# A hybrid decoder layer on one core: branches, output projection and second feed-forward product by seven half-size products each

## Chip, cores and metric

The kernel runs on one core of one Trainium2 chip. The metric is the device time of one execution in microseconds. TensorE is called PE here, VectorE DVE, ScalarE ACT, GpSimd POOL, and SyncE, which issues most DMAs, SP.

## What is computed

One decoder layer over 1024 tokens of width 1024, in float32, batch 1. One input projection feeds two causal mixers (a Mamba-2 scan and an xLSTM matrix memory). Each mixer gives 2048 channels per token. Cut to what the change touches:

```python
y_a = ssd_branch(...)                   # 1024 x 2048, RMS-normed
y_b = mlstm_branch(...)                 # 1024 x 2048, times its output gate
ba, bb = y_a @ w_branch_ssd, y_b @ w_branch_mlstm       # 2048 x 1024 weights
m = sigmoid(g_a) * ba + sigmoid(g_b) * bb
x1 = x + gate1 * (m @ w_out)                            # 1024 x 1024 weight
h = rms_norm(x1) * (1 + scale) + shift
u, g = split(h @ w_ffn_in)                              # width 2816 each
out = rms_norm(x1 + gate2 * ((silu(g) * u) @ w_ffn_out)) * final_norm_w
```

Every factor of a product is held as a pair: a high part rounded to the fast float32 format of PE (f32r) and a low part, the rest. A product takes three matmuls: high x high, high x low, low x high.

## The kernel before, in words

A tile is 128 partitions by 512 or 1024 elements. One matmul has a 128x128 stationary operand and 512 columns, and adds into one of eight PSUM banks of 128x512.

The program has these stages. **Mixers**: the input projection (`gemm`, L276 to L287, 48 matmuls for 128 columns of the weight), convolutions and scans. Their results go to DRAM as `u_d` and `y_d`, the gates (`gate_tile`, L309) as `tg_d`. During the last part, the four heads of the mLSTM scan (L696 to L708), gemms of gates and of the next head stand between the scan's steps.

**Branches and output projection**, in two halves of 512 tokens (L1005 to L1011). For a half, `half_merge` (L805) runs `branch` (L776) twice: for each of 16 blocks of 128 input channels it loads a tile of tokens and a row block of the weight, splits both into pairs, and issues 24 matmuls into all eight banks (L795); `kouter` (L742) interleaves the last two blocks so that the banks end one after the other. DVE then reads each bank, gates it and adds the branches up. `half_out` (L840) multiplies the merged half by `w_out` through `tokgemm` (L828, matmuls L835), and `residual` (L753) adds the rows of x. In the second half of tokens the first branch runs ahead of the operands `f0`, `h0` of the first half (L1007 to L1009).

**Seam**: `feat` (L855) transposes the normed rows, and `ffn_inputs` (L869) forms the sums and differences of the two token halves that the next product needs, 20 pairs in all.

**First feed-forward product** (`ffn1`, L890): for each of 22 blocks `j` of 128 columns, gate and up part together are a 2x2 block product that is computed with seven half-size products (two "head" products `p1`, `p2` and five of sums; matmuls L903). POOL adds up the weights (`wsum`, L894), ACT and DVE split the sums into pairs (`split_pair`, L860: a cast at L863 and a subtraction at L864). The products go to `act_d` in DRAM.

**Second feed-forward product** (`ffn2`, L971): two halves of tokens, each a `tokgemm` over 22 blocks of `act_d` rows and `w_ffn_out` rows, then residual, norm and store.

A scheduler that simulates the program sets the order of the instructions of each engine; tile pools (name, tag, number of buffers) bound how far one part runs ahead of another. All loads in these stages stand on SP's queue, the stores of the mixers and of `act_d` on POOL's.

## Time and profile before

| | us |
|---|---|
| median of 3 runs | 2723.82 |
| lowest and highest run | 2723.11, 2727.63 |
| profiled execution, its own time | 2723.68 |
| its span in the profile | 2722.0 |
| busy in the span: PE | 2605.1 (96%) |
| busy: DVE, ACT, POOL | 1495.7, 1029.5, 434.8 |
| moved by DMA | 323.8 MB, 119 GB/s on average |

The busy time of an engine is the time in which at least one of its instructions runs. Matmuls overlap one another, so PE's busy time is not the sum of their durations. The stretches of the rows below are cut where a stage's first or last matmul stands in the trace: mixers to 1517.4 us, branches and output projection to 1989.0, seam to 2048.3, first feed-forward product to 2460.5, second to 2705.4, tail to 2722.0.

### The profile page before, as it was taken

To read this page: it belongs to the slowest core of one execution; us is meant where nothing else is said; L and a number is where in the kernel's file an instruction comes from. 1 tells how busy PE (TensorE), PEld (TensorE's weight loads), DVE (VectorE), ACT (ScalarE), POOL (GpSimd) and SP (SyncE) were. 2 spreads that over 40 slices of the span, in tenths; PEclk is the share of its full clock that TensorE was granted. 3 is DMA by queue.
4 is the path that set the end of the run, shared out by engine and by line. 5 is a ranking of instruction groups with operands and counts; after the bars stand their busy time and mean duration, and the time that the engine had idled before them with its cause. 6 is when DMAs were issued, how large, how long until landed. Compare 5 with 4: busy or idle time off the path is not lost.

```text
span 2722.0 us, 34219 instructions
## 1 busy us (share of the span) xinstructions
PE 2605.1 (96%) x13279; PEld 2174.1 (80%) x13279; DVE 1495.7 (55%) x2280; ACT 1029.5 (38%) x1785; POOL 434.8 (16%) x410
## 2 busy tenths in 40 slices
...
GB/s 198 100 82 113 104 116 78 113 143 99 133 129 140 88 117 88 61 72 99 55 99 101 162 173 187 177 173 199 136 78 83 78 87 82 82 79 218 137 208 94
DMA packets 261099, 323.80 MB, mean 119 GB/s; under 512 B 16288, under 2 KB 180480, under 8 KB 260936
## 3 DMA queue, kind: packets, MB, share of 16 engines
...
q8 instruction: 104, 1.70, 0.3%
q14 instruction: 59, 0.48, 0.1%
...
## 4 chain that ended last, share of the span: by engine, by line
PE 77%; DVE 7%; DMA 6%; issue 5%; ACT 3%; POOL 3%; SPq 0%; DVEq 0%; POOLq 0%; ACTq 0%
PE mm L284 31%; PE mm L560 7%; PE n L903 6%; PE n L835 5%; PE n L795 4%; PE mm L835 3%; PE sc L835 3%; PE sc L903 3%; PE mm L903 3%; PE n L612 2%; PE mm L795 2%; PE sc L795 2%; DMA raw<-in_w_ffn_in_dram 2%; PE n L630 1%; DMA ab<-acs_d 1%
## 5 line engine op out<-in xcount | busy, mean ns | idle before, releaser
L122 DVE TENSOR_TENSOR wl<-raw,wh 128x1024 fp32r<-128x1024 f32 x250 | 314.6, 1260 | 511.1 <-PE mm L284 155.1
L284 PE MATMUL mm<-hh,wh 128*128 128x512 f32 x1392 | 551.1, 396 | 4.5 <-ACT xf L296 4.3
L284 PE MATMUL mm<-hh,wl 128*128 128x512 f32 x1392 | 549.8, 395 | 0.0
L284 PE MATMUL mm<-hl,wh 128*128 128x512 f32 x1392 | 549.5, 395 | 0.0
L121 ACT CAST wh<-raw 128x1024 fp32r<-128x1024 f32 x250 | 262.1, 1048 | 656.9 <-PE n L835 118.1
L284 PEld LDWEIGHTS mm<-hh,wh 128*128 128x128 f32 x1392 | 262.9, 189 | 57.7 <-ACT xf L296 5.0
L284 PEld LDWEIGHTS mm<-hh,wl 128*128 128x128 f32 x1392 | 262.7, 189 | 51.7 <-issue 0.5
L284 PEld LDWEIGHTS mm<-hl,wh 128*128 128x128 f32 x1392 | 263.0, 189 | 50.8 <-issue 0.2
L304 DVE SCALAR_TENSOR_TENSOR xf<-cr,pk,xf 128x1023 f32<-128x1023 f32 (+2 forms) x120 | 161.9, 1351 | 22.7 <-ACT xf L296 21.6
L795 PE MATMUL n<-us,wh 128*128 128x512 f32 x512 | 159.6, 394 | 7.1 <-DVE am L813 7.1
L903 PE MATMUL n<-t,sw 128*128 128x512 f32 x552 | 140.9, 402 | 16.6 <-ACT sw L863 14.5
L903 PEld LDWEIGHTS n<-t,sw 128*128 128x128 f32 x552 | 105.3, 191 | 43.8 <-ACT sw L863 15.0
L864 DVE TENSOR_TENSOR sw<-ws,sw 128x512 fp32r<-128x512 f32 x88 | 75.9, 867 | 88.2 <-ACT sw L863 87.9
L795 PEld LDWEIGHTS n<-us,wh 128*128 128x128 f32 x512 | 96.8, 190 | 27.9 <-DVE am L813 7.8
L863 ACT CAST sw<-ws 128x512 fp32r<-128x512 f32 x88 | 54.0, 619 | 166.8 <-POOL ws L896 116.4
L835 PE MATMUL n<-wh,ap 128*128 128x512 f32 x352 | 115.1, 389 | 0.0
L464 ACT ACTIVATE ab<-ab,gsum 128x128 f32<-128x128 f32 x256 | 78.5, 389 | 83.2 <-DMA ab<-acs_d 77.7
L795 PE MATMUL n<-us,wl 128*128 128x512 f32 x256 | 99.7, 392 | 0.0
L520 POOL TENSOR_TENSOR Y<-Y,tz 128x512 f32<-128x512 f32 x14 | 33.3, 2396 | 386.3 <-DVE Y L501 222.1
L187 POOL TENSOR_TENSOR sm<-sm,mhalf 128x1 f32<-128x1 f32 x32 | 17.8, 558 | 479.5 <-DVE sm L186 479.5
L896 POOL TENSOR_TENSOR ws<-raw 128x512 f32<-128x512 f32 x44 | 60.0, 1363 | 181.7 <-DMA raw<-in_w_ffn_in_dram 171.0
L560 PE MATMUL mm<-wh,hh 128*128 128x256 f32 x512 | 82.3, 283 | 0.0
(359 smaller groups left out, 4962.4 us busy)
## 6 DMA issues: line engine op xcount, KB each, us to landing
raw<-in_w_in_dram SPq DMA_DIRECT2D x104, 512.0 KB, 4.0
raw<-in_w_ffn_in_dram SPq DMA_DIRECT2D x44, 512.0 KB, 3.8
raw<-in_w_ffn_out_dram SPq DMA_DIRECT2D x44, 512.0 KB, 3.6
raw<-in_w_ada_dram SPq DMA_DIRECT2D x40, 512.0 KB, 3.8
tg_d<-tz POOLq DMA_DIRECT2D x64, 256.0 KB, 2.7
ab<-acs_d SPq DMA_DIRECT2D x32, 512.0 KB, 4.0
raw<-in_w_branch_ssd_dram SPq DMA_DIRECT2D x32, 512.0 KB, 3.7
tgl<-tg_d SPq DMA_DIRECT2D x64, 256.0 KB, 2.8
```

Of the source, the lines that this page charges most:

```text
L121: A.copy(wh, raw)
L122: V.tensor_tensor(wl, raw, f(wh), SUB)
L284: T.matmul(ps, lhsT=ww[:, k, :], rhs=xx[:, halves(hf)], start=n == 0, stop=n == 23)
L304: V.scalar_tensor_tensor(dst[:, sh:], cr[:, :S - sh], cw[:, 3 - sh, ti:ti + 1], dst[:, sh:], MUL, ADD)
L464: A.activation(ab[q][:, e, c], ab[q][:, e, c], AF.Relu, scale=-1.0, bias=acs_t[:, 4 * q + c, h0 + e:h0 + e + 1])
L560: T.matmul(ps[:, c], lhsT=hT[k][x_][:, sl], rhs=ws[k // 4][w_][:, k % 4], start=n == 0, stop=n == 23)
L612: T.matmul(nv(i), lhsT=l_, rhs=r_, start=n == 0, stop=n == len(ops) - 1)
L795: T.matmul(bk[j], lhsT=l_[:, js], rhs=us[:, r_], start=first and n == 0, stop=last and n == 2)
L835: T.matmul(bk[i], lhsT=at[:, l_, tt * P:(tt + 1) * P], rhs=r_[:, halves(nh)], start=first and n == 0, stop=last and n == 2)
L864: e.tensor_tensor(m[:, 1], t, f(m[:, 0]), SUB)
L896: G.tensor_tensor(s, x, y, op)
L903: T.matmul(bank, lhsT=ww[:, k, :], rhs=b[k][:, r_], start=k == 0 and n == 0, stop=k == 3 and n == 2)
```

## The change

The two branches, the output projection and the second feed-forward product are each computed for all 1024 tokens at once as a 2x2 block product by Strassen's scheme: seven products of half the size in each dimension, where the plain way has eight. `b0`/`b1` are the two halves of the input channels, the column halves of a tile are the two halves of tokens, and the weight's quarters A11, A12, A22 and four sums S1 to S4 are its factors.

- `prep_steps` makes the seven factors of a weight as pairs and stores them in DRAM (`fac_d`), through POOL's queue. It is a generator with four steps for each pair of row blocks. Twenty such pairs of blocks (8, 8 and 4 for the three weights of branches and output projection) are handled during the mLSTM heads: two steps behind each gate tile and each late z tile, one in every second chunk of `ml_v`. The 11 of `w_ffn_out` are handled inside the first feed-forward product, behind its even blocks.
- `strassen` runs the seven products in a given order. For each block k it loads a factor pair of 512 KB (`wf`, six in flight, five in the last product), forms the pair of tokens on ACT and DVE (`tok`; with products 2 and 6 it also turns the token tiles into the sums that later products use), and issues 12 matmuls into four banks. The two sets of four banks alternate from product to product.
- The sinks add the products up: DVE reads each bank once or twice, and half-size results are finished where the order completes them.
- In the second branch a token tile takes a gate tile `og` of 512 KB through one buffer.
- In the output projection, rows of the second half take gate and x ahead of the last product (`fold`).
- The first feed-forward product now computes its heads two blocks ahead and its weight sums one block ahead; the operands of the first token half, which stood under the second half's branch, come behind the output projection.

The pools for these stages are new as well. Of the diff, the added code that carries this, without blank lines:

```diff
+    FA = {"A11": 0, "A12": 1, "A22": 2, "S2": 3, "S3": 4, "S4": 5, "S1": 6}
+    fac_d = {n: tc.dram_tile([kk, 7, P, 2, 512], F32, name=f"fac_{n}") for n, kk in (("ssd", 8), ("ml", 8), ("out", 4), ("ffn", 11))}
+    def prep_steps(name, w_d, rawf, pairf):
+        fd = fac_d[name]
+        n = fd.shape[0]
+        def put(r, kk, p0, cnt):
+            wh, wl = pairf()
+            m = cnt * 512
+            A.copy(wh[:, 0:m], r[:, 0:m])
+            V.tensor_tensor(wl[:, 0:m], r[:, 0:m], f(wh[:, 0:m]), SUB)
+            for t, w in enumerate((wh, wl)):
+                G.dma_start(fd[kk, p0:p0 + cnt, :, t, :].rearrange("f p n -> p f n"), f(w[:, 0:m]).rearrange("p (f n) -> p f n", n=512))
+        for kk in range(n):
+            r0, r1 = rawf(), rawf()
+            Q.dma_start(r0, w_d[kk * P:(kk + 1) * P, :])
+            Q.dma_start(r1, w_d[(kk + n) * P:(kk + n + 1) * P, :])
+            put(r0, kk, FA["A11"], 1)
+            yield
+            put(r1, kk, FA["A12"], 2)
+            a11, a21, a12, a22 = r0[:, 0:512], r0[:, 512:], r1[:, 0:512], r1[:, 512:]
+            V.tensor_tensor(a22, a21, a22, ADD)
+            V.tensor_tensor(a21, a11, a21, SUB)
+            V.tensor_tensor(a11, a22, a11, SUB)
+            V.tensor_tensor(a12, a12, a11, SUB)
+            yield
+            put(r0, kk, FA["S2"], 2)
+            yield
+            put(r1, kk, FA["S4"], 2)
+            yield
...
         gemm(w_in[:, col:col + P], epi)
+        for _ in range(2):
+            next(preps, None)
...
                 if i % 2:
                     next(later, None)
+                else:
+                    next(preps, None)
...
+    def phase_a_pair():
+        return [ap.tile([P, 1024], F32R, name=n, tag="cr", bufs=NCR) for n in ("fh", "fl")]
+    preps = chain(*(prep_steps(n, w, lambda: ld("fr"), phase_a_pair) for n, w in
+                    (("ssd", a["w_branch_ssd"][0]), ("ml", a["w_branch_mlstm"][0]), ("out", a["w_out"][0]))))
...
+    def strassen(name, b0, b1, order, sink, wq, nw, tq, nt, tmp, rows=False, odd=0):
+        fd = fac_d[name]
+        n = fd.shape[0]
+        B0, B1 = {}, {}
+        def t0(k):
+            if k not in B0:
+                B0[k] = b0(k)
+            return B0[k]
+        def t1(k):
+            if k not in B1:
+                B1[k] = b1(k)
+            return B1[k]
+        def tok(p, k):
+            if p == 6:
+                t2 = tmp()
+                V.tensor_tensor(t2, t1(k)[:, H_], t0(k)[:, L_], SUB)
+                m = split_pair(t2, tq, "tf", "tf", nt)
+                V.tensor_tensor(t1(k)[:, L_], t1(k)[:, L_], t2, SUB)
+                return m
+            src = {1: lambda: t0(k)[:, L_], 2: lambda: t1(k)[:, L_], 3: lambda: t1(k)[:, H_], 4: lambda: t1(k)[:, L_],
+                   5: lambda: t0(k)[:, L_], 7: lambda: t0(k)[:, H_]}[p]()
+            m = split_pair(src, tq, "tf", "tf", nt)
+            if p == 2:
+                x = t0(k)
+                V.tensor_tensor(x[:, L_], x[:, H_], x[:, L_], SUB)
+                V.tensor_tensor(x[:, H_], t1(k)[:, H_], x[:, H_], SUB)
+            return m
+        wf = {1: "A11", 2: "A12", 3: "S4", 4: "A22", 5: "S1", 6: "S2", 7: "S3"}
+        for q, p in enumerate(order):
+            bk = banks4((q + odd) % 2)
+            def operands(k):
+                w = wq.tile([P, 2, 512], F32R, name="wf", tag="wf", bufs=nw)
+                Q.dma_start(f(w), fd[k, FA[wf[p]]])
+                return w, tok(p, k)
+            def mm(i, k, wt):
+                w, t = wt
+                sl = slice(i * P, (i + 1) * P)
+                st, mv = (t, w) if rows else (w, t)
+                for m, (x, y) in enumerate(((0, 0), (0, 1), (1, 0)) if not rows else ((0, 0), (1, 0), (0, 1))):
+                    T.matmul(bk[i], lhsT=st[:, x, sl], rhs=mv[:, y], start=k == 0 and m == 0, stop=k == n - 1 and m == 2)
+            for k in range(n - 2):
+                wt = operands(k)
+                for i in range(4):
+                    mm(i, k, wt)
+            w2 = [operands(n - 2), operands(n - 1)]
+            for i in range(4):
+                mm(i, n - 2, w2[0])
+                mm(i, n - 1, w2[1])
+                sink(p, i, bk[i])
...
+    def sink_of(ut, tmp, final):
+        U, U3 = {}, {}
+        def sink(p, i, bank):
+            if p == 1:
+                U[i] = ut()
+                A.copy(U[i], bank)
+            elif p == 2:
+                c = tmp()
+                V.tensor_tensor(c, bank, U[i], ADD)
+                final(0, 0, i, c)
+            elif p == 6:
+                V.tensor_tensor(U[i], bank, U[i], ADD)
+            elif p == 7:
+                U3[i] = ut()
+                V.tensor_tensor(U3[i], bank, U[i], ADD)
+            elif p == 5:
+                c = tmp()
+                V.tensor_tensor(c, bank, U3[i], ADD)
+                V.tensor_tensor(U[i], bank, U[i], ADD)
+                final(1, 1, i, c)
+            elif p == 4:
+                V.tensor_tensor(U3[i], bank, U3[i], ADD)
+                final(1, 0, i, U3[i])
+            else:
+                V.tensor_tensor(U[i], bank, U[i], ADD)
+                final(0, 1, i, U[i])
+        return sink
...
+    ORDER = (1, 2, 6, 7, 5, 4, 3)
...
+    def token_tile(pl, src, k, nw, g0=None):
+        t = pl.tile([P, 1024], F32, name="bt", tag="bt", bufs=8)
+        Q.dma_start(t, src[k // 4][(k % 4) * P:(k % 4 + 1) * P, :])
+        if g0 is not None:
+            og = sg.tile([P, 1024], F32, name="og", tag="og", bufs=1)
+            Q.dma_start(og, tg_d[(g0 + k) * P:(g0 + k + 1) * P, :])
+            V.scalar_tensor_tensor(t, og, 1.0, t, ADD, MUL)
+        A.activation(t, t, AF.Copy, scale=nw[:, k:k + 1])
+        return t
...
+    strassen("ssd", lambda k: token_tile(pb0, u_d, k, nw_s), lambda k: token_tile(pb1, u_d, k + 8, nw_s),
+             ORDER, sink_of(ut, ctmp, final_ssd), wq, 6, tq, 5, ctmp)
+    strassen("ml", lambda k: token_tile(pb0, y_d, k, nw_m, 16), lambda k: token_tile(pb1, y_d, k + 8, nw_m, 16),
+             ORDER, sink_of(ut, ctmp, final_ml), wq, 6, tq, 5, ctmp, odd=1)
...
+    def fold(u, i, ci):
+        V.tensor_tensor(u, u, g1[:, halves(ci)], MUL)
+        V.tensor_tensor(u, u, rows_in(po, x_in, 4 + i, ci), ADD)
...
+        elif p == 7:
+            U3[i] = ut()
+            V.tensor_tensor(U3[i], bank, U[i], ADD)
+            V.tensor_tensor(R[i], R[i], U[i], ADD)
+            fold(R[i], i, 0)
...
+    strassen("out", lambda k: am[k], lambda k: am[4 + k], (1, 3, 2, 6, 7, 4, 5), out_sink, wq, 6, tq, 4,
+             lambda: xr_tile(po, "t2"), rows=True, odd=0)
...
+    def head(j):
+        gh, gl = split(wcols(0, j, raw_tile))
+        u1, v = htile("u1", j), htile("v", j)
+        A.copy(u1, product(any_bank(), (gh[:, L_], gl[:, L_]), h0[0:4]))
+        V.tensor_tensor(v, product(any_bank(), (gh[:, H_], gl[:, H_]), h0[4:8]), u1, ADD)
+        tg = e0.tile([P, 512], F32, name="tg", tag="htg", bufs=1)
+        A.activation(tg, v, AF.Tanh, scale=0.5)
+        V.scalar_tensor_tensor(v, tg, 1.0, v, ADD, MUL)
+        return u1, v
+    def wsums(j, rawf):
+        rg, ru = wcols(0, j, rawf), wcols(FF, j, rawf)
+        a11, a12, a21, a22 = rg[:, L_], rg[:, H_], ru[:, L_], ru[:, H_]
+        s1 = ps_.tile([P, 512], F32, name="s1", tag="s1", bufs=1)
+        G.tensor_tensor(s1, a21, a22, ADD)
+        G.tensor_tensor(a21, a11, a21, SUB)
+        G.tensor_tensor(a11, s1, a11, SUB)
+        G.tensor_tensor(a12, a12, a11, SUB)
+        return a11, a21, s1, a22, a12
...
+    h0 = [split_pair(feat(0, k), hlo, "h0", "h0", KD) for k in range(KD)]
+    w5 = [wpair(z) for z in wsums(0, raw_tile)]
+    heads = [head(0), head(1)]
+    tf = {n: [] for n in ("t2", "t3", "t1", "t4", "b22")}
+    for k in range(4):
+        b12, b22, b11, b21, d = feat(1, k), feat(1, k + 4), fx("b11", "fb", 2), fx("b21", "fb", 2), fx("d", "fd", 1)
+        G.tensor_tensor(b11, f(h0[k][:, 0]), f(h0[k][:, 1]), ADD)
+        G.tensor_tensor(b21, f(h0[k + 4][:, 0]), f(h0[k + 4][:, 1]), ADD)
+        def put(n, t):
+            tf[n].append(split_pair(t, hhi, n, "h2", 20))
+        V.tensor_tensor(b11, b12, b11, SUB)
+        V.tensor_tensor(d, b22, b11, SUB)
+        put("t2", d)
+        V.tensor_tensor(b12, b22, b12, SUB)
+        put("t3", b12)
+        put("t1", b11)
+        V.tensor_tensor(b21, b21, d, SUB)
+        put("t4", b21)
+        put("b22", b22)
...
+    preps = prep_steps("ffn", a["w_ffn_out"][0], raw_tile, lambda: [wp.tile([P, 1024], F32R, name=n, bufs=b) for n, b in (("wh", NWH), ("wl", NWL))])
+    for j in range(NFF):
+        u1, v = heads.pop(0)
+        nxt = iter(wsums(j + 1, rw_tile)) if j + 1 < NFF else iter(())
+        five = list(zip(w5, (tf[n] for n in ("t2", "t3", "t1", "t4", "b22"))))
+        w5 = []
...
+        for p in range(5):
+            ps = bk[p] if j == 0 else product(any_bank(), *five[p])
+            for z in nxt:
+                w5.append(wpair(z))
+                break
...
+        if j + 2 < NFF:
+            heads.append(head(j + 2))
+        if j % 2 == 0:
+            for _ in range(4):
+                next(preps, None)
...
+    strassen("ffn", lambda k: act_tile(pb0, k), lambda k: act_tile(pb1, k + 11), ORDER, ffn_sink, wq, 5, tq, 6,
+             lambda: xr_tile(po, "t2"), rows=True, odd=0)
```

What the scheduler makes of it shows in the order of instructions. First SP's queue at the end of the first branch; before, where `uk` is a tile of tokens, `raw` a row block of the branch's weight and `tgl` a gate:

```order
L782 DMA uk<-u_d_86 128x512
L136 DMA raw<-in_w_branch_ssd_dram 128x1024
L782 DMA uk<-u_d_86 128x512
L136 DMA raw<-in_w_branch_ssd_dram 128x1024
L782 DMA uk<-y_d_79 128x512
L802 DMA tgl<-tg_d 128x512
L136 DMA raw<-in_w_branch_ssd_dram 128x1024
```

and after the change, in the second product of the second branch, where `og` is the gate tile of the next tile of tokens, `wf` a factor pair and `tgl` a merge gate:

```order
L905 DMA og<-tg_d 128x1024
L830 DMA wf<-fac_ml 128x1024 x2
L897 DMA tgl<-tg_d 128x512
L830 DMA wf<-fac_ml 128x1024
L905 DMA og<-tg_d 128x1024
L830 DMA wf<-fac_ml 128x1024 x2
L905 DMA og<-tg_d 128x1024
L830 DMA wf<-fac_ml 128x1024 x3
L905 DMA og<-tg_d 128x1024
L830 DMA wf<-fac_ml 128x1024 x2
L905 DMA og<-tg_d 128x1024 x2
L830 DMA wf<-fac_ml 128x1024 x3
```

Before, each block of either half had a gate of half a tile. Now whole gate tiles stand among the factor pairs, six of them around ten pairs, the last two side by side.

Second, DVE in the seam; before, where `x1t` are the rows behind the output projection, `fx` and `d` operands and sums, and the numbered tiles pairs:

```order
L851 TENSOR_SCALAR x1t<-x1t,ssb 128x1024 x2
L876 TENSOR_TENSOR d<-fx 128x512
L880 TENSOR_TENSOR fx<-fx 128x512
L864 TENSOR_TENSOR t_16091<-d,t_16091 128x512
L878 TENSOR_TENSOR d<-fx,d 128x512
L864 TENSOR_TENSOR t_16095<-d,t_16095 128x512
L864 TENSOR_TENSOR t_16099<-fx,t_16099 128x512
L882 TENSOR_TENSOR d<-fx,d 128x512
```

and after, where L154 and L166 are steps of `prep_steps` for `w_ffn_out`, L1068 and L1071 those of a head, and L123 the split of a head's weights:

```order
L123 TENSOR_TENSOR wl<-raw,wh 128x1024
L1068 TENSOR_TENSOR v<-n_16757,u_16741 128x512
L1071 SCALAR_TENSOR_TENSOR v<-tg,v 128x512
L966 TENSOR_SCALAR x1t<-x1t,ssb_15894 128x1024
L154 TENSOR_TENSOR wl<-raw,wh 128x512
L1068 TENSOR_TENSOR v<-mm,u_16780 128x512
L1101 TENSOR_TENSOR b_16826<-f,b_16826 128x512
L1102 TENSOR_TENSOR d<-f,b_16826 128x512
L1104 TENSOR_TENSOR f<-f 128x512
L154 TENSOR_TENSOR wl<-raw,wh 128x1024
L1071 SCALAR_TENSOR_TENSOR v<-tg,v 128x512
L1107 TENSOR_TENSOR b_16827<-b_16827,d 128x512
```

Heads and preparation now stand between the row scalings and among the sums.

Third, DVE in a block of the first feed-forward product; before, where `sw` are pairs of weight sums:

```order
L940 TENSOR_TENSOR v<-n_17114,u_17112 128x512
L968 SCALAR_TENSOR_TENSOR u_16970<-u_16970,up 128x512
L864 TENSOR_TENSOR sw<-ws,sw 128x512
L943 SCALAR_TENSOR_TENSOR v<-tg,v 128x512
L961 TENSOR_TENSOR u_17003<-n_17018,u_17003 128x512
L864 TENSOR_TENSOR sw<-ws,sw 128x512
```

and after, again with L154, L166 and L167 of the preparation:

```order
L1068 TENSOR_TENSOR v<-sc,u_17249 128x512
L154 TENSOR_TENSOR wl<-raw,wh 128x512
L1071 SCALAR_TENSOR_TENSOR v<-tg,v 128x512
L154 TENSOR_TENSOR wl<-raw,wh 128x1024
L1146 TENSOR_TENSOR u_16780<-n_17203,u_16780 128x512
L1133 TENSOR_TENSOR u_17076<-n_17291,u_17076 128x512
L786 TENSOR_TENSOR sw<-rw,sw 128x512
L166 TENSOR_TENSOR raw<-raw 128x512
```

The preparation's operations stand between the evictions of a block.

## Rows read from the trace of the kernel before

**Rows 1.** Busy time by stage; columns: stretch, length, engines, clock, DMA share, GB/s.

```profile
0.00:1517.40 1517.40, 1466.25 (x8391) 1251.76 (x8391) 851.31 (x1470) 650.75 (x1225) 203.32 (x206) 0.99 0.35 106
1517.40:1989.00 471.60, 454.59 (x1952) 368.23 (x1951) 228.39 (x259) 150.09 (x196) 56.29 (x41) 0.98 0.53 172
1989.00:2048.30 59.30, 31.61 (x112) 23.14 (x111) 43.55 (x62) 27.56 (x53) 16.18 (x16) 0.68 0.21 71
2048.30:2460.50 412.20, 409.88 (x1761) 330.64 (x1759) 260.09 (x359) 118.77 (x188) 134.66 (x122) 1.00 0.27 83
2460.50:2705.40 244.90, 242.79 (x1068) 200.34 (x1068) 102.45 (x121) 76.89 (x112) 14.71 (x16) 1.00 0.52 170
2705.40:2722.00 16.60, 0.00 (x0) 0.00 (x0) 9.90 (x13) 5.44 (x14) 9.69 (x10) 0.57 0.34 126
```

**Rows 2.** The same view: two full matmul stretches and one burst of DMA.

```profile
2480.00:2580.00 100.00, 100.00 (x443) 82.84 (x442) 35.83 (x39) 29.40 (x37) 0.00 (x0) 1.00 0.48 155
2200.00:2300.00 100.00, 100.00 (x432) 80.93 (x431) 60.44 (x86) 29.08 (x46) 33.50 (x30) 1.00 0.26 81
2470.00:2480.00 10.00, 10.00 (x46) 8.29 (x45) 3.15 (x4) 1.57 (x3) 0.00 (x0) 1.00 1.03 403
```

**Rows 3.** Matmuls of L795 (first row) and L835 alone, whole span.

```profile
0.00:2722.00 2722.00, 358.19 (x1536) 290.81 (x1536) 0.98 0.38 119
0.00:2722.00 2722.00, 334.23 (x1440) 272.33 (x1440) 0.98 0.38 119
```

**Rows 4.** Groups by line and shape: busy us, mean ns, idle before.

```profile
L864 DVE TENSOR_TENSOR ap<-ta,ap 128x512 fp32r<-128x512 f32 x44 | 30.3, 691 | 30.1 <-ACT ap L863 30.1
L122 DVE TENSOR_TENSOR wl<-raw,wh 128x1024 fp32r<-128x1024 f32 x250 | 314.6, 1260 | 511.1 <-PE mm L284 155.1 <-PE n L835 109.2 <-PE mm L560 79.8
L863 ACT CAST ap<-ta 128x512 fp32r<-128x512 f32 x44 | 27.1, 616 | 18.2 <-DMA ta<-act_d 11.7 <-issue 3.9 <-PE n L835 2.6
L121 ACT CAST wh<-raw 128x1024 fp32r<-128x1024 f32 x250 | 262.1, 1048 | 656.9 <-PE n L835 118.1 <-PE n L795 113.7 <-DMA raw<-in_w_in_dram 90.1
L501 DVE SCALAR_TENSOR_TENSOR Y<-xf,dskip,Y 128x1024 f32<-128x1024 f32 x16 | 20.5, 1281 | 0.5
```

**Rows 5.** Busy time in three stretches of the mixers, columns as above.

```profile
750.00:1517.40 767.40, 763.54 (x4398) 669.52 (x4396) 318.99 (x649) 277.37 (x481) 93.23 (x125) 1.00 0.32 95
100.00:300.00 200.00, 197.85 (x1134) 164.03 (x1133) 142.87 (x216) 102.49 (x205) 10.95 (x7) 1.00 0.34 104
300.00:500.00 200.00, 188.50 (x1047) 156.18 (x1046) 136.37 (x190) 99.95 (x199) 37.22 (x20) 0.98 0.31 98
```

**Rows 6.** DMA issues: count, KB each, median us to landing.

```profile
uk<-y_d SPq DMA_DIRECT2D x32, 256.0 KB, 3.9
y_d<-yb POOLq DMA_DIRECT2D x16, 512.0 KB, 3.5
act_d<-v POOLq DMA_DIRECT2D x22, 256.0 KB, 2.3
```

**Rows 7.** Waits of PE, 1517 to 1989 us: total us, times, longest.

```profile
PE n L795 <- DVE am L813: 7.1, 2, 3.6
```

**Rows 8.** Timeline of DVE at 2012 us: start, duration, instruction.

```profile
2012.70 0.68 DVE L876 TENSOR_TENSOR d<-fx 128x512 f32<-128x512 f32 x1
...
2013.90 0.68 DVE L880 TENSOR_TENSOR fx<-fx 128x512 f32<-128x512 f32 x1
```

**Rows 9.** Group of the row scaling, 1517 to 1990 us.

```profile
L851 DVE TENSOR_SCALAR x1t<-x1t,ssb 128x1024 f32<-128x1024 f32 x4 | 3.0, 748 | 0.0
```

**Rows 10.** Busy time from the projection's end to the first sums' product.

```profile
1989.00:2034.00 45.00, 17.31 (x61) 11.85 (x60) 36.20 (x53) 23.09 (x46) 10.64 (x12) 0.64 0.23 79
```

**Rows 11.** Groups by line and shape in the first feed-forward product.

```profile
L864 DVE TENSOR_TENSOR sw<-ws,sw 128x512 fp32r<-128x512 f32 x88 | 75.9, 867 | 88.2 <-ACT sw L863 87.9
L896 POOL TENSOR_TENSOR ws<-raw 128x512 f32<-128x512 f32 x44 | 60.0, 1363 | 181.7 <-DMA raw<-in_w_ffn_in_dram 171.0 <-DVE v L962 10.7
```

**Rows 12.** Waits of DVE, 2050 to 2460 us: total us, times, longest.

```profile
DVE sw L864 <- ACT sw L863: 82.1, 34, 5.6
```

488 lines of the change are left out of this document (230 added, 258 removed).

## Prediction

> **What bounds the kernel now.** I read the span cut at the stage borders first [rows 1]: for each stage it shows the busy time of every engine, the granted clock and the DMA share. TensorE (PE) is busy 2605 of 2722 us; idle time is concentrated at the start, in the stage of branches and output projection (454.6 of 471.6 us), in the seam before the first feed-forward product (31.6 of 59.3 us, clock 0.68, that is partly at 1.2 instead of 2.4 GHz) and in the last 16.6 us, where it does nothing. VectorE (DVE) is under two thirds busy in every stage but the seam. So matmul count sets the time where PE is full, and DVE sets it in the seam. The profiled execution took 2723.68 us (span 2722.0 and 1.7 around it), the median of the runs 2723.82; the two stand 0.1 us apart, so I write the sum against the profile.
>
> What does one 128x512 matmul cost? Its row says 0.39 us, but these overlap, so I count them in full stretches: the 100 us of the second feed-forward product hold 443, of which one at each end is cut, so 441 in 100 us, 0.2267 us each. In the first product it is 430 in 100 us, 0.2325 us [rows 2]. The branches issue 1536 matmuls; the line of the token-wise products 1440, of which 8x8x3x2 = 384 are the output projection and 22x8x3x2 = 1056 the second feed-forward product [rows 3].
>
> **Matmuls.** A Strassen product set is 7 products x n blocks x 4 row tiles x 3 matmuls, n = 8, 8, 4, 11. That is 672 + 672 + 336 + 924 = 2604 instead of 2976. The 372 that go are worth 372 x 0.2267 = 84.3 us. The rest of the sum asks what is added, and what stays on the path.
>
> **Mixers (to 1517 us): +8 us.** Twenty block pairs are prepared here, beside the mLSTM scan. A pair is one 512-wide and three 1024-wide casts on ACT (0.62 + 3 x 1.05 = 3.8 us [rows 4]), the same subtractions on DVE (0.69 + 3 x 1.26) and four sums of 0.69: 7.2 us of DVE. In all 145 us of DVE and 75 of ACT, and 160 stores on POOL's queue. In 750 to 1517 us DVE has 319 busy, ACT 277 [rows 5]; they become 464 (60%) and 352 (46%). What hides the work is that PE has gemms queued there. Nothing can be gained, as PE idles only 4 us there. For the cost I take the nearest crowded stretches: with DVE at 71% PE idled 2.2 of 200 us, with 68% 11.5 of 200. These ends give 8 and 44 us on 767 us; I take 8, as the first stretch, like the scan, has full gemms behind it. The stores hold the two buffers shared with the convolutions until they land (3.5 us for 512 KB from POOL [rows 6]), beside 48 matmuls, 10.9 us, of gemm for each tile.
>
> **Branches and output projection: -75 us.** Before: 471.6 us for 1920 matmuls, 435.3 us of issue and 36.3 lost. The losses sit where all eight banks are emptied at once: the longest PE wait is for the merge of the banks, 7.1 us in two times [rows 7]. The change works on four banks while DVE empties the other four, so only the first seam stays. After: 1680 x 0.2267 = 380.9, plus 7 (a fifth of 36.3, for five seams before and one such after), plus 9 for gates of the second branch. They are loaded through one buffer: each is a load (3.9 us [rows 6]), a 1024-wide gating on DVE (1.28) and a scaling on ACT (1.05), some 6 us, and the next load stands on SP's queue in front of weights. The order puts the last four only five blocks (13.6 us of PE) ahead of use, against 4 x 6 = 24; 24 - 13.6 is 10, and I take 9. In all 397, against 471.6. DVE in the two branches: 112 subtractions, 64 updates and 120 operations on banks at 0.60 us (three in a row start at 2012.70 to 2013.90, so 1.20 for two steps [rows 8]), and 16 gatings, 200 of 305 us: no bound.
>
> DMA: 112 weight pairs, 32 token tiles, 16 gates of 512 KB and the merge gates, 176 x 0.524 = 92 MB in 305 us, 303 GB/s, where the stage moved 172. A burst in the trace ran at 403 GB/s [rows 2], so it fits on average.
>
> **Seam to the first feed-forward product: +24 us.** Here DVE is the bound, and it gets more. From the first bank of the sixth product of the output projection to the last operand of the first five products, the new order has 96 operations of 512, 8 row scalings (0.75 us [rows 9]) and 7 wide subtractions: 96 x 0.60 + 8 x 0.75 + 7 x 1.26 = 72 us. Among them are three heads where one stood, the operands of the first half (before under the branch), and one block pair's preparation, which the order moved in. Before, DVE was busy 36.2 of 45 us in this place [rows 10], so 80%; 72/0.8 = 90. It begins 33 matmuls (7.5 us) before the projection ends: 83 us, against 59.3. If DVE never waited it would be 65; at the busy share of the whole seam before (43.6 of 59.3, 73%) 91.
>
> **First feed-forward product: -3 us.** In the seam 60 head matmuls are done where 24 were: 36 x 0.2325 = 8.4 us off. DVE per block of 84 matmuls (19.5 us) has 260.1/21 = 12.4 us and gets half a pair, 3.6: 16.0. So PE stays the bound; +5 us for collisions.
>
> The rows show the price of a collision: the same subtraction takes 0.87 us where POOL's weight sums run, 0.69 elsewhere [rows 4, 11]. At that price the added work is 4.5 instead of 3.6 us a block, 16.9 of 19.5: still no bound. Were DVE to stand still for the whole of each of POOL's four sums (1.36 us [rows 11]), that would be 5.5 us a block, and 16.0 + 5.5 = 21.5 passes 19.5 by 2.0: 42 us over 21 blocks in place of my 5. The Trainium skill, "SBUF — State Buffer", "Who interferes with whom", speaks for this harsher case: a DVE instruction with two SBUF inputs and a GpSimd instruction that reads SBUF exclude each other, and the later one waits until the other has ended. The trace bears it out in part: subtractions do get longer beside the sums, by 0.18 us in the mean and not by 1.36. So I keep the 5 and make the other rival 3.
>
> **Second feed-forward product and end: -27 and -4 us.** 924 x 0.2267 = 209.5, plus what the stage lost (244.9 - 239.4 = 5.5), plus 3 for 19 token tiles issued ahead of the sixth weight pair: 218 against 244.9. At the end only the left half of four row tiles is open: 4 x (2 x 0.60 + 2 x 0.69) = 10 us of DVE, started 4 us before PE ends, then square, power and store, 13 against 16.6.
>
> Sum: 8 - 75 + 24 - 3 - 27 - 4 = -77; 2723.7 - 77 = **2647 us**.
>
> **Rivals.**
> 1. The branches run out of data. For: the stage's own ratio, 172 GB/s at a share of 0.53, would be 325 GB/s when full. Two products of the first branch load a token tile with each weight pair, 8.4 MB or 25.8 us against 21.8; two of the second a gate besides, 12.6 MB or 38.7 us. If nothing were fetched ahead: 2 x 4 + 2 x 16.9 = 42 us, 33 beyond my 9: 2680. Against: eight buffers for each half, and 403 GB/s seen.
> 2. The preparation holds up the mixers as in the worse stretch, 44 us instead of 8: 2683. Against: PE idles 0.5% there now.
> 3. DVE stands still during POOL's sums in the first product: 42 us instead of 5, 2684. For: longer subtractions beside them. Against: 0.18 us is all they grow by now.
> 4. Slower: the preparation's subtractions wait in DVE's queue for stores. The low half has two buffers, shared with the heads, so each put may wait for an earlier put's landing on POOL's queue; behind it in DVE stand the evictions, and PE waits for banks. DVE already waits for ACT 82.1 us in the product [rows 12], 3.9 a block: 16.0 + 3.9 = 19.9, full. With two puts a block and 2.3 us for a landing [rows 6] it is 24.5, 5.0 x 21 = 105 us instead of 5: 2747. It begins to count as soon as those waits for ACT persist, and passes the kernel before at 77/21 = 3.7 us a block above 19.5. Against: sums are now made a block ahead, so those waits should shrink, and PE has eight banks of lead.
> That the change does not do what it says is excluded for the count, as the order shows 2604 matmuls; but operands that are sums could run at 0.2325 as in the first product (2604 x 0.0058 = 15 us, 2662), which is within the main case.
>
> **Chances and range.** Main case 0.60, 2612 to 2672: up to 35 below, if seam (65), mixers (0) and gates (0) all come at their cheap ends; up to 25 above. Rival 1 0.14, 2 0.07, 3 0.06, 4 0.10; 0.03 for an end within 0.2% (5.4 us, about what a measurement of this kernel can tell). Faster 0.60 + 0.14 + 0.07 + 0.06 = 0.87, same 0.03, slower 0.10. The range takes in the main case and rivals 1 to 3: 2612 to 2692, with some 0.15 outside.
>
> **What would show it.** Right: 2604 matmuls on the Strassen line at about 0.227 us; PE over 95% busy in the branches without waits at bank changes; projection's end near 1922 us; a seam of 75 to 90 us with DVE as releaser; 19.5 us a block after it; second product of 215 to 220 us. Wrong: PE waits for weight pairs or token subtractions in the branches (rival 1), PE idle among scan steps (2), longer sums on POOL and subtractions over 0.9 us (3), blocks over 20 us with DVE subtractions released by POOL's stores (4).

## The result, and the profile after

The changed kernel takes 2790.12 us (median of 4 runs, 2780.69 to 2794.04) against 2724.95 us: 1.0233 times the time before, 95% interval 1.0205 to 1.0262. Slower by 2.3%, where faster by 2.8% was forecast. Its profiled span is 2792.3 us. The same view as [rows 1], cut at the same places of the program (the first feed-forward product at its very last matmul):

```profile
0.00:1561.40 1561.40, 1479.82 (x8391) 1260.67 (x8391) 981.42 (x1632) 725.75 (x1313) 315.63 (x366) 0.98 0.51 166
1561.40:2001.00 439.60, 395.57 (x1681) 321.37 (x1681) 261.03 (x398) 124.53 (x192) 3.14 (x5) 0.95 0.70 240
2001.00:2079.20 78.20, 42.35 (x148) 29.62 (x148) 62.25 (x85) 42.09 (x74) 29.12 (x31) 0.72 0.43 144
2079.20:2529.40 450.20, 420.30 (x1765) 335.62 (x1763) 357.90 (x450) 151.50 (x231) 200.41 (x208) 0.97 0.64 206
2529.40:2779.30 249.90, 218.93 (x925) 178.31 (x924) 125.81 (x195) 59.93 (x110) 6.45 (x13) 0.92 0.69 229
2779.30:2792.30 13.00, 0.18 (x1) 0.00 (x0) 7.14 (x11) 1.45 (x4) 3.52 (x6) 0.62 0.44 161
```

To compare the first product at equal matmul counts, its matmuls alone, in the kernel before (behind the projection's end, two stretches):

```profile
1989.00:2069.60 80.60, 43.97 (x168) 34.55 (x169) 0.77 0.26 84
2069.60:2463.60 394.00, 391.50 (x1681) 315.55 (x1680) 1.00 0.26 83
```

and after:

```profile
2001.00:2112.00 111.00, 53.96 (x168) 38.30 (x169) 0.74 0.45 146
2112.00:2529.40 417.40, 396.09 (x1681) 317.20 (x1680) 0.98 0.65 210
```

So, by stage, measured against forecast: mixers +44 (forecast +8); branches and projection 439.6 - 471.6 = -32 (-75); from the projection's end to the first product's end (111.0 + 417.4) - (80.6 + 394.0) = +54 (+24 - 3 = +21); second product 249.9 against 242.0, from 2463.6 to 2705.6 (245 in [rows 1], which begin 3 us earlier), +8 (-27); end -3 (-4). Their sum is, but for rounding, the +70 of the spans. Four stages miss, each by 33 to 43 us.

The 372 matmuls are gone: the counts are 1680 and 924 (the rows have one more, cut at a border). With 372 x 0.2267 = 84 us less to issue, PE is busy 2557.2 us against 2605.1. So it idles 118 us more than before (235.1 against 116.9), and the matmuls that stay take it 36 us more. The granted clock fits this second part: its mean over the span is 0.960 against 0.984, and the 96 matmuls of the 41.7 us product below keep PE busy for 26.4 us at a granted clock of 0.86, where others take 21.8 at 1.00.

These are products of the Strassen scheme (first and fourth product of the first branch, second of the second branch, third of the projection with the wait behind it, then the wait before and the first two products of the second feed-forward product):

```profile
1561.90:1588.10 26.20, 22.34 (x96) 17.97 (x97) 17.93 (x28) 16.00 (x23) 0.33 (x1) 1.00 1.01 382
...
1639.90:1661.70 21.80, 21.80 (x98) 18.06 (x97) 7.79 (x11) 5.76 (x9) 0.00 (x0) 1.00 0.79 261
1748.70:1790.40 41.70, 26.42 (x98) 19.70 (x96) 21.38 (x30) 10.93 (x14) 0.00 (x0) 0.86 0.60 202
...
1924.10:1952.10 28.00, 11.12 (x50) 8.87 (x48) 10.74 (x17) 6.30 (x15) 0.00 (x0) 0.77 0.47 151
2529.40:2538.30 8.90, 0.18 (x1) 0.00 (x0) 2.19 (x4) 1.21 (x2) 1.08 (x2) 0.71 0.89 301
2538.30:2582.10 43.80, 34.72 (x132) 27.74 (x133) 24.53 (x37) 10.91 (x19) 0.00 (x0) 0.83 0.90 347
2582.10:2626.10 44.00, 31.71 (x133) 25.31 (x132) 14.28 (x22) 7.81 (x18) 0.00 (x0) 0.87 0.58 179
```

The fourth product is what was planned: 96 matmuls in 21.8 us, PE full. Longer than planned are the first three products of the first branch (26.2, 25.7 and 26.1 us), the second and third of the second branch (41.7 and 24.9; its first takes 21.8), the third and fourth of the projection (28.0 and 15.6, where 10.9 was planned) and the first three of the last set (43.8, 44.0 and 33.4 for 29.9). In them token tiles are loaded, turned into sums, or both.

Two chains show how. In the second branch's second product, time runs over the gates, one after the other through the single buffer, the next load issued only when DVE has used the last:

```profile
1753.56 4.45 DMA og<-tg_d
...
1758.03 1.24 DVE bt L906
...
1759.28 5.07 DMA og<-tg_d
...
1764.38 1.24 DVE bt L906
```

Four such rounds last from 1753.6 to 1776.3 us. The product's matmuls take 33.8 us, 12 more than planned, the lower clock included. The other 8 of the 41.7 stand behind them: DVE adds up that product's banks, waits 4.04 us for a merge gate (`tgl`), and the sums of tokens for the next product stand behind this in its queue. At the same place of the first branch:

```profile
1610.73 3.33 DMA tgl<-tg_d
...
1614.09 0.69 DVE tgl L915
...
1616.64 2.07 PE mm L838 x4
```

Of the mixers' 44 us PE idles 30 and is busy 14 more for the same 8391 instructions. There the waits from 740 to 1561 us have new entries, on ACT, DVE and SP's queue. Three of those of the preparation (total us, times, longest):

```profile
ACT fh L153 <- DMA fac_ssd<-fh: 27.1, 10, 5.7
DVE fl L154 <- DMA fac_ssd<-fl: 38.8, 14, 8.1
SPq L161 <- DVE fl L154: 66.6, 13, 8.0
```

A cast or subtraction of the preparation waits in its engine's queue until an earlier store has landed, and a preparation load waits on SP's queue with the gemms' weight loads behind it. The largest single loss shows in the chain at 904 us:

```profile
903.71 5.99 DMA fac_ssd<-fh
...
909.78 0.59 ACT cr L332
910.37 0.69 ACT xf L333
...
911.10 4.21 PE mm L321 x9
```

A store of the preparation lands, ACT may then evict a convolution's bank (`cr`, whose two buffers the pairs share), and PE goes on. In this stretch PE did next to nothing, and its granted clock, 1.00 before, fell and stayed lower in the next 13 us (48 matmuls, which take 10.9 us at full clock):

```profile
880.00:894.00 14.00, 13.13 (x63) 10.95 (x62) 6.95 (x10) 3.31 (x4) 3.94 (x6) 1.00 0.92 311
894.00:911.00 17.00, 0.70 (x4) 0.24 (x2) 9.09 (x11) 5.21 (x8) 2.60 (x5) 0.62 0.79 266
911.00:924.00 13.00, 12.90 (x48) 10.51 (x49) 5.86 (x6) 4.47 (x8) 0.73 (x1) 0.84 0.25 82
```

### The profile page after: what moved, and what is told of

Its sections match the earlier page's. It is cut to its first block, busy times and chain, and to the rows that moved or that the text cites. A ratio compares the mean times of both kernels' runs of the same rounds, so it can differ in the third digit from the quotient of the medians.

```text
span 2792.3 us, 34946 instructions
## 1 busy us (share of the span) xinstructions
PE 2557.2 (92%) x12907; PEld 2125.6 (76%) x12907; DVE 1795.5 (64%) x2768; ACT 1105.2 (40%) x1923; POOL 558.3 (20%) x627
## 4 chain that ended last, share of the span: by engine, by line
PE 59%; DMA 13%; DVE 12%; issue 8%; POOL 4%; ACT 3%; SPq 0%; POOLq 0%; DVEq 0%; ACTq 0%
PE mm L321 25%; PE n L838 10%; PE mm L601 7%; PE mm L838 5%; PE sc L838 4%; PE n L655 2%; DVE sw L786 1%; DMA raw<-in_w_ffn_out_dram 1%; DVE wl L154 1%; DMA fac_ffn<-wl 1%; DMA raw<-in_w_ffn_in_dram 1%; PE n L530 1%; DMA xr<-in_x_dram 1%; PE n L673 1%; PE n L1046 1%
## 5 line engine op out<-in xcount | busy, mean ns | idle before, releaser
L123 DVE TENSOR_TENSOR wl<-raw,wh 128x1024 fp32r<-128x1024 f32 x126 | 158.6, 1259 | 153.2 <-PE mm L321 69.2
L122 ACT CAST wh<-raw 128x1024 fp32r<-128x1024 f32 x126 | 131.7, 1045 | 217.8 <-DMA raw<-in_w_in_dram 69.3
L786 DVE TENSOR_TENSOR tf<-bt,tf 128x512 fp32r<-128x512 f32 x162 | 110.6, 690 | 159.9 <-ACT tf L785 159.9
L785 ACT CAST tf<-bt 128x512 fp32r<-128x512 f32 x162 | 99.8, 621 | 255.0 <-PE sc L838 130.1
L154 DVE TENSOR_TENSOR fl<-fr,fh 128x512 fp32r<-128x512 f32 (+1 forms) x80 | 88.2, 1102 | 133.7 <-DMA fac_ssd<-fl 46.1
L838 PE MATMUL n<-tf,wf 128*128 128x512 f32 x672 | 157.8, 393 | 9.7 <-ACT tf L785 7.8
L838 PEld LDWEIGHTS n<-tf,wf 128*128 128x128 f32 x672 | 127.3, 190 | 37.7 <-ACT tf L785 8.2
L838 PE MATMUL n<-wf,tf 128*128 128x512 f32 x540 | 129.5, 398 | 23.8 <-ACT tf L785 16.9
L838 PEld LDWEIGHTS n<-wf,tf 128*128 128x128 f32 x540 | 103.7, 193 | 47.0 <-ACT tf L785 17.4
L838 PE MATMUL mm<-wf,tf 128*128 128x512 f32 x360 | 97.9, 404 | 26.0 <-ACT tf L785 16.0
```

The lines of the kernel that those rows point to most:

```text
L122: A.copy(wh, raw)
L123: V.tensor_tensor(wl, raw, f(wh), SUB)
L154: V.tensor_tensor(wl[:, 0:m], r[:, 0:m], f(wh[:, 0:m]), SUB)
L785: A.copy(m[:, 0], t)
L786: V.tensor_tensor(m[:, 1], t, f(m[:, 0]), SUB)
L838: T.matmul(bk[i], lhsT=st[:, x, sl], rhs=mv[:, y], start=k == 0 and m == 0, stop=k == n - 1 and m == 2)
```

## Experiments

The kernel before was run beside each group on the same chip; its time stands with the group. Each variant ran once, sums_dve eight times. What one run can tell shows in the mixers: half_w and xr_ring below leave them as they are, with the instructions of every engine in the same order, and they end at 1554.8 and 1553.0 us there, at 1561.4 in the changed kernel. The row of xr_ring:

```profile
0.00:1553.00 1553.00, 1473.47 (x8391) 1254.03 (x8391) 986.57 (x1632) 726.23 (x1312) 313.60 (x366) 0.98 0.52 167
```

So some 8 us between two runs of the mixers show nothing. In the variants that change the preparation, the scheduler also chose another order of instructions from soon after its first step on; their differences include that.

### What the preparation costs (before: 2721.28 us)

**no_prep.** `for kk in range(n)` in `prep_steps` becomes `range(1)`, and every block loads block 0's factors (`fd[0, ...]`). Expected:

> The preparation of weight factors is left out for all pairs of row blocks but the first of each weight; every block of a product then loads the first block's factors, so loads and matmuls stay as in the changed kernel. If the preparation is what lengthens the mixers and the first feed-forward product: last input-projection stage ends near 1520 us instead of 1561, the stretch from the projection's last matmul to the first feed-forward product's last goes from 528 to 470 to 485 us, blocks of 84 matmuls at 19.1 to 19.5 us throughout; branches with projection (440 us) and second product (250 us) stay, since their loss would be their own loads; about 2700 us. Rival, that the preparation's traffic reaches into the branches: these shorten too, by 10 us or more.

**no_store.** `for t, w in enumerate((wh, wl) if kk == 0 else ()):` before the stores, loads as above. Expected:

> The casts, subtractions and sums of the preparation stay, its stores are left out but for the first pair of blocks of each weight (which all blocks then load). Theory queue (the pair's two buffers are held until a store has landed, and ACT and DVE wait for that with everything behind them): mixers end by 1525 us, blocks of the first product 19.1 to 19.5. Theory work (the added casts and subtractions themselves): mixers still end after 1545, and blocks with a preparation stay at 21 to 25 us. Theory traffic (140 MB more of stores slow the weight loads): as theory queue.

Measured 2718.78 and 2736.79 us. The stages of no_prep (mixers, branches with projection, then the first product in two stretches):

```profile
0.00:1520.90 1520.90, 1469.00 (x8391) 1253.94 (x8391) 877.13 (x1496) 668.50 (x1244) 219.63 (x230) 0.99 0.37 118
1520.90:1961.40 440.50, 396.93 (x1681) 322.40 (x1681) 260.69 (x398) 124.25 (x193) 3.15 (x5) 0.95 0.68 240
1961.40:2069.70 108.30, 65.17 (x233) 46.76 (x232) 87.04 (x114) 53.35 (x92) 40.92 (x41) 0.76 0.46 147
2069.70:2453.40 383.70, 383.70 (x1681) 315.11 (x1679) 252.78 (x336) 110.22 (x173) 135.66 (x119) 1.00 0.34 107
```

and of no_store (mixers, and the last of these stretches):

```profile
0.00:1531.70 1531.70, 1474.25 (x8391) 1257.48 (x8391) 983.76 (x1632) 724.82 (x1312) 223.16 (x230) 0.99 0.41 129
2076.90:2473.40 396.50, 388.80 (x1681) 313.47 (x1679) 319.47 (x416) 140.97 (x213) 138.88 (x119) 1.00 0.42 130
```

The preparation costs 1561 - 1521 = 40 us in the mixers and 417 - 384 = 34 in the first product. Of these its casts, subtractions and sums cost 11 and 13, its stores 30 (21 if the mixers end at 1553) and 21. The mixers of no_store lie between the two expectations. Branches, seam (108 of 111 us) and second product do not change: their losses are their own, and a changed kernel with free factors is only level with the kernel before.

### Which part of a store (before: 2721.28 and 2735.40 us)

**const_store.** Stores read `hT[0]` (later `h0[0]`) in place of the pair. Expected:

> The preparation's work and as many stores of the same size on the same queue stay, but the stores read a tile that nobody rewrites (a high part of the normed input in the mixers, of the first operand in the first product), so no buffer waits for them; the stored factors are thus not those of the weights. Theory queue: mixers end by 1530 us and blocks of the first product are within 0.5 us of those without stores. Theory traffic: mixers end after 1550, and landing times of weight loads stay at 4.6 us and above. Theory work: mixers end after 1545.

Measured 2911.54 us, but not what it was made for: with nothing to wait for, the scheduler issued these stores at the program's start. PE's first 3852 instructions take 830 us there and 724 in the changed kernel, and the first cast of the preparation stands at 724 instead of 617 us: all of that is lost ahead of any preparation. It tells nothing about the stores' place in the mixers, but there such stores cost time although no buffer waits for them.

**thin_store.** The stores behind block 0's write `[:, :, 0:32]` of each 512 columns. Expected:

> Every store of the preparation stays in its place and is waited for, but writes 32 of each 512 columns (the first pair of blocks in full; all blocks load that pair's factors). 1531 us is where the mixers end without stores, 1560 with them, and the blocks 2 to 21 of the first product take 396 and 417. If the bytes are what costs (they slow the loads of weights, and they make the landing that a buffer waits for long): mixers end by 1538, blocks by 401. If it is the fixed part of each landing, waited for in ACT's and DVE's queues however little is written: mixers end after 1548, blocks above 408.

**late_const.** A store of one column of the pair, then a full one from `hT[0]`. Expected:

> Each store of the preparation is split: a store of one column frees the pair buffer, and behind it on the same queue the full store of the same size reads a tile that nobody rewrites. So the bytes move at about the old place, and a buffer is held for one short landing only. The stored factors are not those of the weights. If the held buffers cost the time: mixers end by 1545 us, blocks 2 to 21 of the first product by 405 us. If it is the traffic itself that slows the loads: mixers end after 1552, blocks above 412, landing of the weight loads in the mixers still over 4.4 us.

Measured 2778.51 and 2845.22 us. Thin stores:

```profile
0.00:1553.00 1553.00, 1480.70 (x8391) 1260.29 (x8391) 985.22 (x1634) 728.36 (x1317) 315.59 (x366) 0.99 0.42 129
2108.00:2513.00 405.00, 390.32 (x1680) 316.38 (x1679) 333.46 (x416) 141.62 (x213) 187.92 (x197) 0.99 0.43 133
```

So 1553 - 1532 = 21 of the 30 us in the mixers stay though next to nothing is written, and about 9 of 21 in the first product. As unchanged mixers ended at 1553 too, the mixers show no gain at all from the smaller bytes, although weight loads there land after 4.2 us in the median (from 740 to 1540 us), as before the change, and after 5.8 in the changed kernel: in the mixers the fixed part of a store counts more than its bytes. In late_const the mixers end at 1598 and the blocks take 433 us, and the weight loads land after 4.8 us. By its own marks that run speaks for the traffic; but it issues twice as many stores, and thin stores keep the cost without the traffic. Neither theory explains both runs, and what a store costs in the mixers is not taken apart further.

### Which wait (before: 2730.57 us for the first, 2724.86 for the others)

**fr_pool.** `G.dma_start` for the two loads of a pair. Expected:

> The changed kernel with one edit: the preparation loads its weights from POOL's queue instead of SP's. If weight loads of the input projection are late because they stand on SP's queue behind a preparation load that waits for its buffer (SP waited 151 us there between 740 and 1560 us): mixers end by 1550 us instead of 1560, blocks 2 to 21 of the first product in 412 us or less. If only ACT's and DVE's waits for stores count: mixers end at 1555 to 1562 as before.

**store_act.** `A.dma_start` for the stores. Expected:

> The changed kernel with the preparation's stores issued from ACT's queue instead of POOL's. Theory POOL's queue (stores that wait there for casts hold up the gates' stores and the small powers of the scan, which loads on that queue made worse): mixers end by 1545 us, blocks 2 to 21 of the first product by 408. Theory of buffers alone: 1552 to 1562, and 412 to 420. Rival, that ACT now waits for DVE's subtraction before it can issue a low half's store: mixers end after 1565.

**own_ring.** Pairs get `tag="fp", bufs=2`; `NXF` 10 becomes 8. Expected:

> The changed kernel with two buffers of their own for the pairs of the preparation in the mixers, in place of the two that convolutions use too; the room comes from the mixers' ring of wide tiles, eight instead of ten. If the convolutions' evictions waiting for stores in the shared ring cause the loss (the 16.8 us that PE stood at 894 us, with the clock halved behind it): mixers end by 1540 us instead of 1560. If the waits of the preparation's own casts in ACT's and DVE's queues cause it, whoever owns the buffers: still 1550 to 1562. If eight wide tiles are too few: later than 1565.

**prep_late.** `preps` is created behind `ml_scan(1, ...)`, three steps a hook. Expected:

> The changed kernel with the preparation in the mixers begun after the second head's scan, where the loads for the modulation vectors and the first late gates are over, at three steps instead of two behind each gate. 32 of the 43 us are lost between 740 and 950 us, where all of these meet. If it is that crowd: mixers end by 1540. If each step costs its share wherever it stands: 1555 or later.

Measured 2814.52, 2777.20, 2812.38 and 2886.13 us; mixers end at 1578, 1562, 1587 and 1658 us. No single change helps the mixers. Loads on POOL's queue make it worse by 17 us, stores on ACT's queue change nothing there (they save 10 us in the first product, 407.4 instead of 417.4, the mark set for POOL's queue). Own buffers at the price of two wide tiles lose 26, of which 9 are lost ahead of the first preparation step (matmul 1681 of the input projection starts at 614 instead of 605 us); by its third mark that run says that eight wide tiles are too few, and so nothing about the buffers. And that crowd is not needed: the same preparation, its casts between 965 and 1633 us instead of 617 and 1458, and three steps a hook instead of two, costs 141 instead of 44 us. What grows is waiting, not work (DVE is busy 988 us in the mixers, against 981 in the changed kernel). Which of the queues starts it stays open; buffers of their own without a price elsewhere were not tried.

### The loads and the row buffers (before: 2721.28 and 2735.40 us)

**half_w.** `if k % 2 == 0:` before a factor's load, the next block uses the same pair. Expected:

> A factor pair is loaded for every second block only and used for two, which takes 256 KB of 512 KB from each block's weight traffic and changes the products. If the first products of each stage are bound by the rate of their loads (386 GB/s at full matmul rate where tokens and weights are both loaded, 290 with half the weights): the first two products of the second feed-forward product take 33 us or less each instead of 44, and the wait in front of them shrinks from 9 to 6 us or less; the first three products of the first branch lose 3 us instead of 12. Second product of the second branch, 41.7 us now: if the one gate buffer with its chain of load, gating, scaling binds it, it stays above 35 us; if the rate binds it, it falls to 27 or less. Total 2755 to 2770 us. If loads bind nothing: no change.

Measured 2749.47 us. Wait before and first two products of the second feed-forward product:

```profile
2496.40:2505.00 8.60, 0.34 (x2) 0.00 (x0) 2.35 (x4) 1.09 (x2) 1.08 (x2) 0.75 0.89 305
2505.00:2537.80 32.80, 32.59 (x132) 26.73 (x133) 24.68 (x38) 11.05 (x19) 0.00 (x0) 0.91 0.99 396
2537.80:2580.30 42.50, 31.74 (x134) 25.35 (x132) 13.63 (x21) 7.76 (x17) 0.00 (x0) 0.87 0.35 115
```

The first product falls from 43.8 to 32.8 us at 396 GB/s: its loads bound it. The second product of the second branch falls from 41.7 to 26.1 us: its matmuls take 21.8, the chain over the gates is gone, and 4 us stay behind them. So the single buffer need not cost time. With half as many factor loads around the gates on SP's queue, and six pairs that serve twelve blocks and so reach further ahead, rate and lateness are not told apart here; but at a DMA share of 0.60 the changed kernel's product as a whole was not short of rate. The first branch's first three products still lose 8 of their 13 us: the first falls from 26.2 to 22.4, the two behind it, which moved 181 and 174 GB/s in the changed kernel, lose almost what they lost. The wait before (8.6) and the second product (42.5, at 115 GB/s) do not change, so something else holds them. For the second product the next run shows it. No run takes away the wait before; in the changed kernel its chain goes from the first product's last matmul, at 2529 us, over the load of a broadcast row (6.17 us) to the token tiles behind it on SP's queue.

**xr_ring.** `tag="xin", bufs=6` (3 in the last product) for rows of x; projection's `wq` 6 becomes 4, last `tq` 6 becomes 5. Expected:

> Rows of x and x1 that the sinks of output projection and second feed-forward product read get buffers of their own (six and three) in place of four shared with the sinks' temporaries; to make room the projection's factor ring goes from six to four, the last product's token ring from six to five. If the four shared buffers make DVE wait for one load after the other, with the next product's token sums behind it: the third product of the projection, 28.0 us with the wait behind it, falls to 18 or less, and the seam between second and third product of the second feed-forward product from 7.8 to 4 or less; about 2780 us. If the wait is for the load itself, whatever is issued ahead: no change, 2792.

Measured 2761.43 us. Projection's third product, and the last stage's second, each with the wait behind it:

```profile
1915.80:1934.60 18.80, 11.15 (x50) 8.85 (x48) 10.76 (x17) 6.33 (x15) 0.00 (x0) 0.91 0.65 214
2556.50:2593.30 36.80, 30.45 (x134) 24.55 (x132) 15.08 (x23) 8.48 (x19) 0.00 (x0) 1.00 0.65 197
```

28.0 becomes 18.8 (18 or less was expected), 44.0 becomes 36.8: four buffers for rows, temporaries and squares made DVE wait for one row load after the other, with the next product's token sums behind it in its queue. Of the 19 us by which the total is under the 2780 expected, 8 stand in the mixers, which this run leaves unchanged.

### Do the parts add up? (before: 2726.81 us)

**free_factors.** no_prep, half_w and xr_ring together. Expected:

> The three losses named so far taken away together: one pair of row blocks prepared per weight, each factor pair loaded for every second block only and used for two, rows with their own buffers. The matmuls stay 2604 and the other work of the products stays, but the factors are not the right ones. If the parts add up, from no_prep (span 2717): 9 us less in the projection, 7 in the second product and 10 in the seam from the rows' buffers, 20 in the branches and 11 in the second product from the halved loads: 2655 to 2675 us. Rival, that the losses cover for one another and another bound (DVE in the branches) stands behind them: 2690 or more.

Measured 2677.09 us, span 2675.4. Mixers, branches with projection, then the first product in two stretches and the second:

```profile
0.00:1526.00 1526.00, 1472.00 (x8391) 1256.18 (x8391) 875.78 (x1496) 668.01 (x1244) 215.89 (x230) 0.99 0.38 118
1526.00:1939.80 413.80, 391.15 (x1681) 319.82 (x1681) 262.21 (x402) 123.40 (x195) 2.99 (x6) 0.97 0.51 170
1939.80:2044.00 104.20, 67.47 (x233) 49.31 (x233) 84.26 (x111) 52.78 (x90) 41.16 (x39) 0.74 0.43 140
2044.00:2427.60 383.60, 383.60 (x1681) 315.21 (x1679) 251.74 (x336) 110.39 (x173) 135.22 (x120) 1.00 0.35 109
2427.60:2662.50 234.90, 217.32 (x926) 177.84 (x924) 127.03 (x198) 60.07 (x110) 8.67 (x12) 0.95 0.47 162
```

Just above what was expected. The three causes are 2792.3 - 2675.4 = 117 of the 147 us between the forecast and the profiled execution (2794.0, the slowest of four that lie 13 us apart). Against the forecast, the other 30 stand in the branches with the projection (413.8 for 397, +17) and in the second product (234.9 for 242 - 27 = 215, +20), while the mixers fit and the time from the projection's end to the first product's end is 8 us shorter (487.8 for 474.6 + 21). They are not taken apart by runs.

### Other ways to make the factors (before: 2735.40, 2730.57, 2724.86, 2726.81 us)

**sums_v** stores only the four sums as float32; a product loads 256 KB and splits it:

```diff
-                Q.dma_start(f(w), fd[k, FA[wf[p]]])
+                Q.dma_start(raw, factor(wf[p], k))
+                A.copy(w[:, 0], raw)
+                V.tensor_tensor(w[:, 1], raw, f(w[:, 0]), SUB)
```

> Only the four sums of a pair of row blocks are stored, as plain float32 (1 MB instead of 3.5 MB), computed on POOL; the products load 256 KB of a factor, of the weight itself for A11, A12 and A22, and ACT and DVE split it there (0.62 us on ACT, 0.69 on DVE for each block of 2.72 us). If stores and casts of the preparation and the rate of the loads are the causes: mixers end by 1535 us, branches and projection in 420 us or less, blocks 2 to 21 of the first product in 400 or less, second product by 242; total 2690 to 2725 us. Rival, that DVE becomes the bound (60 to 68% busy in the branches, 22% more): branches and projection stay at 440 or more with PE waiting for DVE.

2746.65 us: better than the change, not than before. The input projection's last matmul still starts at 1544 us (1560 in the changed kernel, 1517 before) without any cast, and branches with projection take 438 us: DVE, which has the splits as well, is busy 45 of the 50 us from 1670 us, but PE is busy 48 of them, so that DVE became the bound is not shown.

**sums_pool** adds xr_ring and `G.dma_start` for the loads. Expected:

> Sums alone stored and factors split in the products, as in the earlier run of that name, and the preparation wholly on POOL: its loads, sums and stores stand on POOL's queue, so no other engine waits for its buffers. With the rows' own buffers in the projection (five) and the last product (three). If the rest of the loss in the mixers (1544 us with sums, 1517 before) was SP's queue: mixers end by 1527. Projection's third product at 19 us or less. Branches and projection 425 to 430 us, first product's blocks 2 to 21 in 390 to 400, second product 237; total 2700 to 2720. Rival, that the added loads and stores cost by their mere traffic: mixers end after 1538.

**sums_early** prepares the last weight in the mixers as well. Expected:

> As sums_pool, but the eleven pairs of the last weight are prepared during the mixers too, two steps to a pair. Nothing is prepared in the first feed-forward product, so its blocks 2 to 21 take 384 us as they do without preparation; mixers end within 5 us of sums_pool if POOL's queue has room. Rival: POOL's queue is full and the gate stores behind it hold ACT, mixers end 15 us later or more.

**sums_alt** splits every second factor with `G.tensor_tensor`. Expected:

> As sums_early, but every second block's factor is split by POOL instead of DVE (POOL has next to nothing to do in the branches). If DVE's work bounds the crowded products (first product of the second branch 23.9 us, its second 30.4, the first branch's fifth 25.5): branches and projection 8 us or more shorter than in sums_early. Rival: DVE's operations get longer beside POOL's (0.87 instead of 0.69 us beside the weight sums), and the gain is under 3 us.

2751.24, 2745.15 and 2777.50 us; the last gemm matmul starts at 1553, 1564 and 1560. POOL alone as the preparer is no cure, and branches with projection go from 434 to 460 us with POOL's splits. POOL's own operations are slow, and DVE's get longer beside them, as the rival had it: the splits of weights by little (0.71 us), those of tokens by a third. By the groups of that stretch, POOL's splits and DVE's of tokens, and the latter in sums_early:

```profile
L826 POOL TENSOR_TENSOR wf<-wr,wf 128x512 fp32r<-128x512 f32 x70 | 137.0, 1960 | 310.9 <-ACT wf L825 310.9
L773 DVE TENSOR_TENSOR tf<-bt,tf 128x512 fp32r<-128x512 f32 x93 | 86.4, 933 | 25.8 <-ACT tf L772 25.8
...
L773 DVE TENSOR_TENSOR tf<-bt,tf 128x512 fp32r<-128x512 f32 x96 | 65.8, 687 | 17.2 <-ACT tf L772 17.2
```

**sums_noffn2** keeps Strassen for branches and projection and has the last product in its old form; **sums_dve** is the same with DVE adding up the weights. Expected:

> Strassen for branches and projection only, with sums stored from SP-loaded tiles, factors split in the products and the rows' own buffers; second feed-forward product as before the change, nothing prepared in the first. From the parts measured: mixers 1545, branches and projection 433, to the third block 98, blocks 2 to 21 384, second product 242 and 17 of tail: about 2720 us, if the stages do not act on one another; that is what the kernel before takes. Rival: the second product's old form, without operands ready when the first ends, starts later, 2730 or more.

> As sums_noffn2, but DVE instead of POOL adds up the weights in the mixers. There the chain of the mixers went from a preparation load over four sums on POOL to the scan's small power that stood behind them on POOL's queue, to DVE, ACT and PE. If POOL's queue is what costs: mixers end by 1535 instead of 1545, total 2715 to 2724, level with the kernel before. Rival, that the preparation's loads and stores cost in SP's queue and as traffic, whoever adds: mixers end at 1542 to 1552, total 2728 to 2738.

2733.68 us, and 2733.23 us against 2726.81 in three rounds, 1.0020 times before (95% interval 1.0010 to 1.0031). In sums_noffn2 the chain of the mixers at 957 us ran over POOL: a preparation load (5.15 us), its sums from 962 us on, stores, and behind them, at 970 us, the scan's small power, for which ACT and PE waited.

But with the sums on DVE the last gemm matmul starts at 1547, with them on POOL at 1545 us. Whoever adds, the loss of some 28 us stays; that chain was where it showed, not its cause. No version found that computes the layer is faster than the kernel before; no_prep and free_factors work with wrong factors.

## Why the prediction was wrong

Four terms of its sum failed: the mixers' 8 us, in which the stores were put at nothing; the 16 us of idle PE in branches and projection; the 5 us of collisions in the first product; and the 3 us of late loads in the second. All four also took matmuls at 0.2267 or 0.2325 us, as if PE came back from a gap at full clock; it spent 36 us more on the matmuls that stayed.

**Matmuls: right.** 2604 at 0.227 us. The undisturbed products take 21.8 and 29.9 us.

**"Mixers: +8 us": wrong, and the step is the choice of its row.** The cost was taken from the stretch with full gemms behind it, whose DVE is as busy. Rival 2 named the other end, 44 us, which is what came, by chance: the share of DVE was the wrong scale for both. The work itself costs 11 us (no_store); 21 to 30 are stores and the waits they put into queues, and the text had priced the stores at nothing, as they stood "beside 48 matmuls, 10.9 us, of gemm for each tile".

**"Branches and output projection: -75": wrong by 43.** Allowed were 16 us of idle PE. Measured are 58 beyond 1680 matmuls. The gates' 9 were 12 (33.8 against 21.8 us; rival 1 had this place): the round of some 6 us was right, a load of 3.7 to 5.1 and 1.24 of gating, but four such rounds ran while PE waited for their tokens. 8 more stand behind that product, at a merge gate. 17 were not listed: the third product of the projection, where "only the first seam stays" left out that rows of x are loaded in the sinks, through four shared buffers; 5 more lie in the product behind it and 3 in the second branch's third. Another 13 lie in the first three products of the first branch (78 against 65 us). The first of them was priced by an average ("so it fits on average"): it needs 16 x 0.524 MB in 21.8 us, 385 GB/s, and took 26.2 at 382. The other two were not short of rate; ahead of the third PE waits behind a merge gate, as shown above.

**"Seam: +24": nearly right.** To the same count of 84 matmuls it took 78.2 us against 61.1 before, +17; the forecast less its 8.4 us of heads is +16. DVE was busy 62.3 of 78.2 us, the assumed 80%. What followed was not forecast: the next 84 matmuls took 32.8 us in place of 19.5, as PE waited 7.7 us for a pair of weight sums; without any preparation they still took 30.1.

**"First product: -3 us", with +5 for collisions: wrong by 32.** Counted from the same 84 matmuls on, it took 450.2 us against 413.5, +37 for the 5 (the 8.4 us of heads are in the seam's count above). 13 of these are the 84 matmuls just named, which take almost as long without a preparation. The blocks behind them took 417.4 us against 394.0; without a preparation they take 384, so the preparation costs 34, 21 for its stores and 13 for its work. Rival 4 had the mechanism, stores that hold pairs with ACT and DVE waiting in line, but priced at 105 us, and only in part: DVE waited for these stores six times, 11.5 us in all. Rival 3, DVE standing still beside POOL's sums, came for single operations, and the prediction had set it aside by a mean. The weight sums' subtractions took 0.89 us in the mean, against 0.87 [rows 11], but in both kernels most take 0.68, and about a quarter before and a fifth after take 1.1 us or more. One of them and the POOL sum beside it (two views, DVE and POOL):

```profile
2272.73 2.08 DVE L786 TENSOR_TENSOR sw<-rw,sw 128x512 fp32r<-128x512 f32 x1
...
2272.96 1.29 POOL L1080 TENSOR_TENSOR rw<-rw 128x512 f32<-128x512 f32 x1
```

The preparation's wide subtractions meet the sums as well: 1.62 us in the mean in this product, against 1.26 [rows 4]. What this costs PE no run shows; at 335.5 of 417.4 us DVE as a whole was not full.

**"Second product: -27": wrong, and here a sum was not made.** "3 for 19 token tiles issued ahead of the sixth weight pair": 19 x 0.524 MB at the 403 GB/s of [rows 2] are 24.7 us, against 5 x 2.7 us of matmuls, 11 late instead of 3. The stage lost 249.9 - 209.5 = 40 us: some 9 in the wait before it, 14 in each of its first two products and 4 in the third. Halved factor loads give back 11 (half_w), rows with their own buffers 7 (xr_ring); for the rest no run names a cause.

The range fell with this: its main case put every unlisted wait at zero, and the cases of loss were taken as exclusive, where all came together. Slower by 0.10 was for one mechanism; four half-sized ones did it.
